# Partition sums issued four steps into a stage, squares added in two steps, each bank's residual ahead of the previous bank's low parts, and head squares taken a bank at a time

## The chip, the cores and the metric

The kernel runs on one core of a Trainium2 chip. The engines are named as in the profile: PE is TensorE (PEld its weight loads), DVE VectorE, ACT ScalarE, POOL GpSimd and SP SyncE, which issues most of the DMAs. The metric is the device time of one execution in microseconds (us). The median of the runs before is compared with that of the runs after.

## What is computed

The reference is a trunk of four layers on 256 positions of width 1024, in float32. Cut to what matters:

```python
for i in range(DEPTH):                       # 4 layers
    h = _rmsnorm(x, norm1[i])
    m = (retention, moba, diff)[i % 3](h)    # layers 0 and 3 are retention
    x = x + m
    x = x + _squared_relu_mlp(_rmsnorm(x, norm2[i]), w_up[i], w_down[i])

def _rmsnorm(x, w):
    return x * lax.rsqrt(jnp.mean(x * x, axis=-1, keepdims=True) + EPS) * w
```

The two attention mixers normalise queries and keys per head; the differential one (layer 2) also normalises each head's output of 128 columns. The retention mixer projects to queries, keys, values and a gate.

## The kernel before

The residual stream stays in the core's memory as `X`, with features on the 128 partitions: 8 chunks of 128 features by 256 positions. Every weight is streamed from HBM once, in raw tiles of 1 MB, each cut into two pieces. To keep float32 accuracy at the speed of the `fp32r` type, each operand is split in a high part (ACT copies it to `fp32r`: `whi`, `xhi`) and a low part (DVE subtracts the high part: `wlo`, `xlo`), and a product is three matmuls, high x high, high x low, low x high (`passes`, lines 333 to 335). A piece takes 12 matmuls of 512 columns (`mm_b`) or 24 of 256 columns (`mm_a`, `mm_o`).

`advance` splits pieces ahead of their use: when piece n is taken, the pieces up to n+4 have been put on ACT's and DVE's queues. Every engine works through its queue in program order, so where a step is issued decides what stands in front of it. Small steps are put off by hand: `later(n, f)` runs `f` at the n-th `tick` from now, and a tick comes once per piece, and once more inside the first piece of a stage.

There are eight norms, one ahead of each mixer (`norm1`) and one ahead of each MLP (`norm2`). A norm is spread over the border of two stages:

- `finish` ends a stage. PE completes the four PSUM banks `acc` one after the other; for each bank DVE adds it to `X` (behind an MLP it first scales it by `r2b` into `sc`), ACT writes `xhi` of its two chunks and DVE `xlo` (`norm_part`), and ACT squares the two chunks into a tile `sq` (`squares`). The new stage's matmuls work on `xhi` and `xlo` without the norm's factor, which is a number per position and is multiplied in later.
- `rms`, one tick into the next stage, adds the four `sq` tiles on DVE and then the two halves of the sum.
- `rms_sum`, one tick later, sums over the partitions by a matmul with ones into the PSUM tile `ms`. For an MLP DVE turns it into `r2b` (lines 316 and 317), which is used when that MLP finishes. For a mixer DVE makes `me` and its reciprocal `r2`, and POOL the inverse square root `r` in 13 small steps (`rsqrt`).

In the attention layers `qk_norm` needs `me` (through the POOL step `qem`). It makes sums of squares per head (DVE's `TENSOR_REDUCE`), POOL makes the factors `qf`, DVE scales the queries (`qn`), and PE transposes them (`qkT`) when the second group of four pieces is done. In layer 2 `av_diff` makes the outputs of four pairs of heads in two PSUM banks (`od`); ACT takes the squares and their sums over each 128 columns, eight instructions with an accumulator each, and POOL makes factors of them.

Of the kernel before, what the change touches and what calls it, by code (L numbers as in the profile page):

```python
# [9 lines left out]
F32 = mybir.dt.float32  # L10
F32R = mybir.dt.float32r
I32 = mybir.dt.int32
AF = mybir.ActivationFunctionType
OP = mybir.AluOpType
AX = mybir.AxisListType

P = 128
# [14 lines left out]
def trunk(ctx, tc, x_t, cols, rel_bias, w_up, w_down, ret_w_in, ret_w_out, moba_w_in, moba_w_out,  # L32
# [3 lines left out]
    PE, ACT, DVE, POOL = nc.tensor, nc.scalar, nc.vector, nc.gpsimd  # L36
# [7 lines left out]
    mp = ctx.enter_context(tc.tile_pool(name="mp", bufs=1))  # L44
# [21 lines left out]
    def later(n, fn, *a):  # L66
        clock[1] += 1
        pending.append((clock[0] + n, ORDER.get(fn.__name__, 3), clock[1], fn, a))

    def run_due():  # L70
        while True:
            due = [p for p in pending if p[0] <= clock[0]]
            if not due:
                return
            p = min(due, key=lambda p: p[:3])
            pending.remove(p)
            p[3](*p[4])

    def tick():
        clock[0] += 1  # L80
        run_due()
# [4 lines left out]
    def hi_lo(i, a, b, narrow):  # L86
        n = a * b
        hi = wp.tile([P, n], F32R, tag="hi", name="whi", bufs=NPC)
        odd = i % 2
        lo = wp.tile([P, n + (32 if odd else 96)], F32R, tag="lo%d" % (i % NPC), name="wlo", bufs=1)  # L90
        o = 0 if odd == narrow else (32 if odd else 96)
        return (t.rearrange("p (a b) -> p a b", a=a) for t in (hi, lo[:, o:o + n]))
# [35 lines left out]
    for l in range(DEPTH):  # L128
        j = l // 3
# [20 lines left out]
    def load_raw(part=0, of=1):  # L150
        i = nxt[0]
        if i >= len(specs):
            return
        src, a, b = specs[i]
        if part == 0:
            raws[i] = rp.tile([P, a, b], F32, tag="raw", name="raw", bufs=NRAW)
        hs = slice(part * (a // of), (part + 1) * (a // of))
        nc.sync.dma_start(raws[i][:, hs, :], src[:, hs, :])
        if part == of - 1:
            nxt[0] += 1  # L160
# [40 lines left out]
    def take():  # L201
        p = pieces.pop(nxt[2])
        nxt[2] += 1
        return p
# [13 lines left out]
    junk = const.tile([P, 512], mybir.dt.bfloat16, name="junk")  # L218
# [40 lines left out]
    def wn(l, which, k):  # L259
        c = 32 * which + l * KC + k  # L260
        return W[:, c:c + 1]
# [18 lines left out]
    st = {}  # L280
# [7 lines left out]
        st["hi"] = hi[:, oh:oh + n].rearrange("p (k s) -> p k s", k=KC)  # L288
        st["lo"] = lo[:, ol:ol + n].rearrange("p (k s) -> p k s", k=KC)

    def norm_part(l, which, q):

        for k in (2 * q, 2 * q + 1):
            ACT.activation(st["hi"][:, k, :], X[:, k, :], AF.Copy, scale=wn(l, which, k))
        for k in (2 * q, 2 * q + 1):
            DVE.scalar_tensor_tensor(st["lo"][:, k, :], X[:, k, :], wn(l, which, k),  # L296
                                     st["hi"][:, k, :].bitcast(F32), op0=OP.mult, op1=OP.subtract)

    def squares(q):
        sq = mp.tile([P, 512], F32, tag="pe", name="sq", bufs=9)  # L300
        ACT.activation(sq, X[:, 2 * q:2 * q + 2, :].rearrange("p k s -> p (k s)"), AF.Square)
        st["sq", q] = sq

    def rms(which):

        ss = st["sq", 0]
        for q in range(1, 4):
            DVE.tensor_tensor(ss, ss, st["sq", q], op=OP.add)
        DVE.tensor_tensor(ss[:, :S], ss[:, :S], ss[:, S:], op=OP.add)
        later(1, rms_sum, which, ss)  # L310

    def rms_sum(which, ss):
        ps = aux_bank("ms")
# [37 lines left out]
    def first_qk(ps):  # L351

        for i in range(2):
            pieces[i] = tuple(hi_lo(i, 4, S, True))

        def turn(pr):
            norm_part(0, 0, pr)
            hi, lo = pieces[pr // 2]
            kk = slice(pr % 2 * 2, pr % 2 * 2 + 2)
            raw = raws[0][:, 2 * pr:2 * pr + 2, :]  # L360
            ACT.activation(hi[:, kk], raw, AF.Copy)
            DVE.tensor_tensor(lo[:, kk], raw, hi[:, kk].bitcast(F32), op=OP.subtract)

        def meet(pr):

            ks = (2 * pr, 2 * pr + 1)
            hi, lo = pieces[pr // 2]
            for k in ks:
                for m in range(2):
                    mc = slice(m * P, (m + 1) * P)  # L370
                    pc = ps[:, m * S:(m + 1) * S]
                    PE.matmul(pc, lhsT=hi[:, k % 4, mc], rhs=st["hi"][:, k, :], start=k == 0 and m == 0, stop=False,
                              skip_group_check=True)
                    PE.matmul(pc, lhsT=hi[:, k % 4, mc], rhs=st["lo"][:, k, :], start=False, stop=False,
                              skip_group_check=True)
            for k in ks:
                for m in range(2):
                    mc = slice(m * P, (m + 1) * P)
                    PE.matmul(ps[:, m * S:(m + 1) * S], lhsT=lo[:, k % 4, mc], rhs=st["hi"][:, k, :], start=False,
                              stop=k == KC - 1 and m == 1, skip_group_check=True)  # L380

        turn(0)
        turn(1)
        for pr in range(4):
            meet(pr)
            if pr == 3:
                for q in range(4):
                    squares(q)
            if pr < 2:
                turn(pr + 2)  # L390
            if pr == 2:
                nxt[1] = nxt[2] = nxt[3] = 2
                load_raw()
                for _ in range(2):
                    split_piece()
                    split_lo()
            if pr:
                tick()
        for i in range(2):
            pieces.pop(i)  # L400
# [32 lines left out]
    def finish(srcs, mlp_out, nxt_norm):  # L433
        advance(4, 4)
        pcs = [take() for _ in srcs]
        if nxt_norm is not None:
            norm_new(nxt_norm[1] == 1)
        for q in range(4):
            for i, (pc, src) in enumerate(zip(pcs, srcs)):
                for c in (2 * q, 2 * q + 1):  # L440
                    mm_o(c, pc, src, False, i == len(srcs) - 1)
            xs = X[:, 2 * q:2 * q + 2, :]
            ps = st["acc"][q].rearrange("p (k s) -> p k s", k=2)
            if mlp_out:
                sc = mp.tile([P, 2, S], F32, tag="t2k", name="sc", bufs=4)
                DVE.tensor_tensor(sc, ps, r2b.unsqueeze(1).to_broadcast([P, 2, S]), op=OP.mult)
                DVE.tensor_tensor(xs, xs, sc, op=OP.add)
            else:
                DVE.tensor_tensor(xs, ps, xs, op=OP.add)
            if nxt_norm is None:  # L450
                nc.sync.dma_start(out.rearrange("(k p) s -> p k s", p=P)[:, 2 * q:2 * q + 2, :], xs)
            else:
                norm_part(nxt_norm[0], nxt_norm[1], q)
                squares(q)
            tick()
        if nxt_norm is not None:
            later(1, rms, nxt_norm[1])
# [194 lines left out]
    def attention(l):  # L652
# [139 lines left out]
        def av_diff(b):  # L792
            so = small("so", [P, 4, 2])
            sums = small("s1", [P, 4, 2])
            banks = []
            for i in range(4):
                p = b * 4 + i
                if i % 2 == 0:
                    banks.append(aux_bank("od").rearrange("p (i q v) -> p i q v", i=2, q=2))
                ps = banks[-1][:, i % 2]  # L800
                s = PT[p][0]
                vs = slice(p * P, (p + 1) * P)
                PE.matmul(ps[:, 0], lhsT=s[:, 0:P], rhs=V[0][:, vs], start=True, stop=True)
                PE.matmul(ps[:, 1], lhsT=s[:, P:S], rhs=V[0][:, vs], start=True, stop=False)
                PE.matmul(ps[:, 1], lhsT=s[:, S:GL], rhs=V[1][:, vs], start=False, stop=True)
                if i % 2 == 1:
                    for j in (i - 1, i):
                        for qt in range(2):
                            ACT.activation(junk[:, :P], banks[-1][:, j % 2, qt], AF.Square,
                                           accum_out=so[:, j, qt:qt + 1])  # L810
                POOL.tensor_copy(sums[:, i, :], SM[p][:, :, 0])
            m = small("om", [P, 4, 2])
            POOL.tensor_tensor(m, sums, sums, op=OP.mult)
            POOL.tensor_scalar(m, m, EPS, None, op0=OP.mult)
            POOL.tensor_scalar(so, so, 1.0 / P, None, op0=OP.mult)
            POOL.tensor_tensor(m, m, so, op=OP.add)
            f = small("of", [P, 4, 2])
            rsqrt(f, m, "of", POOL)
            later(2, od_scale, b, banks, f)
# [100 lines left out]
```

## Time and profile before

| | |
|---|---|
| median of 3 runs | 1374.78 us (1373.95 to 1375.21) |
| the profiled execution | 1373.68 us |
| its span, first to last instruction | 1371.9 us |
| PE busy | 1331.1 us, 97% of the span |
| DVE, ACT, POOL busy | 868.2, 684.9, 110.7 us |
| DMA traffic | 242.53 MB, mean 177 GB/s |

The profile shows one execution; its time lies 1.1 us under the median of the runs, and 1.8 us lie outside its span. Busy time counts a matmul from its start to its modelled end, and matmuls overlap, so that a busy PE may still be running slowly: the granted clock, in shares of full speed, says whether it does.

### The profile page before, as it was taken

To read this page: it belongs to the slowest core of one execution; us is meant where nothing else is said; L and a number is where in the kernel's file an instruction comes from. 1 tells how busy PE (TensorE), PEld (TensorE's weight loads), DVE (VectorE), ACT (ScalarE), POOL (GpSimd) and SP (SyncE) were. 2 spreads that over 40 slices of the span, in tenths; PEclk is the share of its full clock that TensorE was granted. 3 is DMA by queue.
4 is the path that set the end of the run, shared out by engine and by line. 5 is a ranking of instruction groups with operands and counts; after the bars stand their busy time and mean duration, and the time that the engine had idled before them with its cause. 6 is when DMAs were issued, how large, how long until landed. Compare 5 with 4: busy or idle time off the path is not lost.

```text
span 1371.9 us, 23860 instructions
## 1 busy us (share of the span) xinstructions
PE 1331.1 (97%) x10035; PEld 1249.1 (91%) x10035; DVE 868.2 (63%) x1237; ACT 684.9 (50%) x1002; POOL 110.7 (8%) x295
## 2 busy tenths in 40 slices
PE   8999999999989999999989999999899999999998
PEld 6888899999977789999967789999888889999998
DVE  7666647555577857555568676555666665665555
ACT  5454435444445754444456754544445444454442
POOL 1111100000041000000031100000030111000000
PEclk9999999999999999999999999999999999999999
DMA  8544554555554336555543337555555545365551
GB/s 299 166 167 162 186 185 167 203 204 195 185 197 141 123 128 215 185 192 203 190 144 133 123 126 243 184 185 186 176 167 171 184 157 195 115 236 203 202 184 63
DMA packets 141691, 242.53 MB, mean 177 GB/s; under 512 B 4160, under 2 KB 89824, under 8 KB 141584
## 3 DMA queue, kind: packets, MB, share of 16 engines
q1 hardware_dynamic: 139760, 237.78, 50.5%
q0 software_dynamic: 752, 2.33, 0.6%
q8 instruction: 78, 1.28, 0.4%
q10 hardware_dynamic: 1072, 0.90, 0.2%
q14 instruction: 29, 0.24, 0.1%
HBM read 239.92 MB, written 1.07 MB: 176 GB/s over the span
## 4 chain that ended last, share of the span: by engine, by line
PE 88%; DVE 6%; ACT 3%; DMA 1%; issue 1%; SPq 0%; DVEq 0%; ACTq 0%
PE acc L333 10%; PE acc L334 10%; PE acc L335 10%; PE up L335 8%; PE up L333 8%; PE up L334 8%; PE vg L333 4%; PE vg L335 4%; PE vg L334 4%; PE qkv L333 3%; PE qkv L334 3%; PE qkv L335 3%; PE qk L333 2%; PE qk L334 2%; PE qk L335 2%; DVE xlo L296 2%
## 5 line engine op out<-in xcount | busy, mean ns | idle before, releaser
L186 DVE TENSOR_TENSOR wlo<-raw,whi 128x1024 fp32r<-128x1024 f32 (+1 forms) x448 | 526.9, 1215 | 96.6 <-ACT whi L176 95.5
L176 ACT ACTIVATE whi<-raw 128x1024 fp32r<-128x1024 f32 (+1 forms) x448 | 451.9, 1052 | 94.1 <-PE acc L334 58.1
L335 PE MATMUL up<-xhi,wlo 128*128 128x256 f32 x1024 | 283.8, 277 | 1.2 <-DVE wlo L186 1.2
L333 PE MATMUL up<-xhi,whi 128*128 128x256 f32 x1024 | 284.3, 278 | 0.0
L334 PE MATMUL up<-xlo,whi 128*128 128x256 f32 x1024 | 283.4, 277 | 0.0
L334 PE MATMUL acc<-uu,whi 128*128 128x256 f32 x1024 | 282.7, 276 | 0.0
L333 PE MATMUL acc<-uu,whi 128*128 128x256 f32 x1024 | 282.6, 276 | 0.0
L335 PE MATMUL acc<-uu,wlo 128*128 128x256 f32 x1024 | 282.6, 276 | 0.0
L335 PEld LDWEIGHTS up<-xhi,wlo 128*128 128x128 f32 x1024 | 193.0, 188 | 1.8 <-DVE wlo L186 1.8
L334 PEld LDWEIGHTS up<-xlo,whi 128*128 128x128 f32 x1024 | 193.1, 189 | 0.1
L333 PEld LDWEIGHTS up<-xhi,whi 128*128 128x128 f32 x1024 | 193.0, 188 | 0.1
L333 PEld LDWEIGHTS acc<-uu,whi 128*128 128x128 f32 x1024 | 192.2, 188 | 0.0
L335 PEld LDWEIGHTS acc<-uu,wlo 128*128 128x128 f32 x1024 | 192.2, 188 | 0.0
L334 PEld LDWEIGHTS acc<-uu,whi 128*128 128x128 f32 x1024 | 192.2, 188 | 0.0
L466 DVE SCALAR_TENSOR_TENSOR u<-up,u 128x512 f32<-128x512 f32 x64 | 44.2, 690 | 207.4 <-ACT u L465 207.4
L465 ACT ACTIVATE u<-up 128x512 f32<-128x512 f32 x64 | 38.3, 599 | 255.7 <-PE up L335 255.7
L333 PE MATMUL acc<-oh,whi 128*128 128x256 f32 x384 | 106.9, 278 | 0.0
L334 PE MATMUL acc<-ol,whi 128*128 128x256 f32 x384 | 106.1, 276 | 0.0
L335 PE MATMUL acc<-oh,wlo 128*128 128x256 f32 x384 | 106.1, 276 | 0.0
L333 PE MATMUL vg<-whi,xhi 128*128 128x512 f32 x256 | 100.5, 393 | 0.0
L335 PE MATMUL vg<-whi,xlo 128*128 128x512 f32 x256 | 99.7, 390 | 0.0
L334 PE MATMUL vg<-wlo,xhi 128*128 128x512 f32 x256 | 99.7, 390 | 0.0
(220 smaller groups left out, 1931.3 us busy)
## 6 DMA issues: line engine op xcount, KB each, us to landing
raw<-in_w_up_dram SPq DMA_DIRECT2D x64, 1024.0 KB, 5.4
raw<-in_w_down_dram SPq DMA_DIRECT2D x64, 1024.0 KB, 5.7
raw<-in_ret_w_in_dram SPq DMA_DIRECT2D x45, 1024.0 KB, 5.2
raw<-in_ret_w_out_dram SPq DMA_DIRECT2D x16, 1024.0 KB, 4.8
raw<-in_moba_w_in_dram SPq DMA_DIRECT2D x12, 1024.0 KB, 5.2
raw<-in_diff_w_in_dram SPq DMA_DIRECT2D x12, 1024.0 KB, 5.2
raw<-in_moba_w_out_dram SPq DMA_DIRECT2D x4, 1024.0 KB, 4.9
raw<-in_diff_w_out_dram SPq DMA_DIRECT2D x4, 1024.0 KB, 4.9
```

Source lines behind the costliest of these rows:

```text
L176: ACT.activation(hi[:, part], half[:, part], AF.Copy)
L186: DVE.tensor_tensor(lo[:, part], half[:, part], hi[:, part].bitcast(F32), op=OP.subtract)
L296: DVE.scalar_tensor_tensor(st["lo"][:, k, :], X[:, k, :], wn(l, which, k), st["hi"][:, k, :].bitcast(F32), op0=OP.mult, op1=OP.subtract)
L333: PE.matmul(ps, lhsT=ah, rhs=bh, start=first, stop=False, skip_group_check=True)
L334: PE.matmul(ps, lhsT=ah, rhs=bl, start=False, stop=False, skip_group_check=True)
L335: PE.matmul(ps, lhsT=al, rhs=bh, start=False, stop=last, skip_group_check=True)
L465: ACT.activation(u, ps, AF.Relu)
L466: DVE.scalar_tensor_tensor(u, ps, 0.0, u, op0=OP.max, op1=OP.mult)
```

## The change

The change has four parts, in five places of the code. (1) `rms_sum` is issued two ticks later, at the fourth tick of a stage in place of the second. (2) `rms` adds three of the four tiles of squares; the last one and the two halves are added a tick later, by the new `rms_fold`. (3) `norm_part` is cut in `norm_hi` and `norm_lo`, and in `finish` the low parts of a bank are issued behind the residual of the next bank. (4) `av_diff` squares a whole bank on ACT with no accumulator, and DVE sums each 128 columns.

```diff
-    def norm_part(l, which, q):
+    def norm_hi(l, which, q):
 
         for k in (2 * q, 2 * q + 1):
             ACT.activation(st["hi"][:, k, :], X[:, k, :], AF.Copy, scale=wn(l, which, k))
+
+    def norm_lo(l, which, q):
         for k in (2 * q, 2 * q + 1):
             DVE.scalar_tensor_tensor(st["lo"][:, k, :], X[:, k, :], wn(l, which, k),
                                      st["hi"][:, k, :].bitcast(F32), op0=OP.mult, op1=OP.subtract)
@@
         ss = st["sq", 0]
-        for q in range(1, 4):
+        for q in (1, 2):
             DVE.tensor_tensor(ss, ss, st["sq", q], op=OP.add)
+        later(1, rms_fold, which, ss)
+
+    def rms_fold(which, ss):
+        DVE.tensor_tensor(ss, ss, st["sq", 3], op=OP.add)
         DVE.tensor_tensor(ss[:, :S], ss[:, :S], ss[:, S:], op=OP.add)
-        later(1, rms_sum, which, ss)
+        later(2, rms_sum, which, ss)
@@
             else:
-                norm_part(nxt_norm[0], nxt_norm[1], q)
+                norm_hi(*nxt_norm, q)
+                if q:
+                    norm_lo(*nxt_norm, q - 1)
                 squares(q)
+                if q == 3:
+                    norm_lo(*nxt_norm, q)
             tick()
@@
                 if i % 2 == 1:
-                    for j in (i - 1, i):
-                        for qt in range(2):
-                            ACT.activation(junk[:, :P], banks[-1][:, j % 2, qt], AF.Square,
-                                           accum_out=so[:, j, qt:qt + 1])
+                    sq = mp.tile([P, 512], F32, tag="t2k", name="sq", bufs=4)
+                    ACT.activation(sq, banks[-1].rearrange("p i q v -> p (i q v)"), AF.Square)
+                    DVE.tensor_reduce(so[:, i - 1:i + 1, :].rearrange("p i q -> p (i q)"),
+                                      sq.rearrange("p (h d) -> p h d", d=P), axis=AX.X, op=OP.add)
```

How the instructions move is shown at three places. First, PE's queue at the start of layer 1's attention. The number behind `whi` tells the piece: 3967 is the first of the stage, 3995 the second. Before:

```order
L333 MATMUL qkv_4139<-whi_3967,xhi_4002 128x512
L334 MATMUL qkv_4139<-wlo_3968,xhi_4002 128x512
L335 MATMUL qkv_4139<-whi_3967,xlo_4001 128x512
L320 MATMUL ms_4156<-ones_90,sq_4028 128x1 x2
L333 MATMUL qkv_4138<-whi_3995,xhi_4002 128x512
L334 MATMUL qkv_4138<-wlo_3996,xhi_4002 128x512
```

And of the change, where `whi_4156` is the third piece of the stage and `whi_4160` the fourth:

```order
L339 MATMUL qkv_4139<-whi_4156,xhi_4002 128x512
L340 MATMUL qkv_4139<-wlo_4157,xhi_4002 128x512
L341 MATMUL qkv_4139<-whi_4156,xlo_4001 128x512
L326 MATMUL ms_4204<-ones_90,sq_4026 128x1 x2
L339 MATMUL qkv_4138<-whi_4160,xhi_4002 128x512
L340 MATMUL qkv_4138<-wlo_4161,xhi_4002 128x512
```

The sum over the partitions stood behind 12 matmuls of the stage and stands behind 36. In the stages that begin with `mm_a` (the MLPs and layer 3) it stood behind 24 matmuls and stands behind 72; in layer 0's mixer it moves 36 matmuls back.

Second, DVE's queue from the last two banks of layer 0's MLP to the start of layer 1's attention. Before:

```order
L446 TENSOR_TENSOR sc<-acc,r2b 128x512
L447 TENSOR_TENSOR X<-X,sc 128x512
L296 SCALAR_TENSOR_TENSOR xlo<-X,W,xhi 128x256 x2
L446 TENSOR_TENSOR sc<-acc,r2b 128x512
L447 TENSOR_TENSOR X<-X,sc 128x512
L296 SCALAR_TENSOR_TENSOR xlo<-X,W,xhi 128x256 x2
L630 TENSOR_TENSOR gs<-gps,msk 16x384
L308 TENSOR_TENSOR sq<-sq 128x512 x3
L309 TENSOR_TENSOR sq<-sq 128x256
L323 TENSOR_SCALAR me<-ms 128x2
L326 RECIPROCAL r_4161<-me 128x2
L186 TENSOR_TENSOR wlo<-raw,whi 128x1024 x6
```

And of the change:

```order
L298 SCALAR_TENSOR_TENSOR xlo<-X,W,xhi 128x256 x2
L453 TENSOR_TENSOR sc<-acc,r2b 128x512
L454 TENSOR_TENSOR X<-X,sc 128x512
L298 SCALAR_TENSOR_TENSOR xlo<-X,W,xhi 128x256 x4
L641 TENSOR_TENSOR gs<-gps,msk 16x384
L310 TENSOR_TENSOR sq<-sq 128x512 x2
L314 TENSOR_TENSOR sq<-sq 128x512
L315 TENSOR_TENSOR sq<-sq 128x256
L186 TENSOR_TENSOR wlo<-raw,whi 128x1024 x5
L329 TENSOR_SCALAR me<-ms 128x2
L332 RECIPROCAL r_4209<-me 128x2
L186 TENSOR_TENSOR wlo<-raw,whi 128x1024
```

The four additions of squares still stand between the last low parts of `X` and the first low part of a weight piece; `me` has moved behind five weight pieces.

Third, DVE's queue at the start of layer 0's MLP. Before:

```order
L296 SCALAR_TENSOR_TENSOR xlo<-X,W,xhi 128x256 x2
L308 TENSOR_TENSOR sq<-sq 128x512 x3
L309 TENSOR_TENSOR sq<-sq 128x256
L316 TENSOR_SCALAR r2b<-ms 128x256
L317 RECIPROCAL r2b<-r2b 128x256
L186 TENSOR_TENSOR wlo<-raw,whi 128x1024 x4
L466 SCALAR_TENSOR_TENSOR u<-up,u 128x512
L471 TENSOR_TENSOR uu<-u,uu 128x512
L186 TENSOR_TENSOR wlo<-raw,whi 128x1024 x2
```

And of the change:

```order
L310 TENSOR_TENSOR sq<-sq 128x512 x2
L314 TENSOR_TENSOR sq<-sq 128x512
L315 TENSOR_TENSOR sq<-sq 128x256
L186 TENSOR_TENSOR wlo<-raw,whi 128x1024 x4
L477 SCALAR_TENSOR_TENSOR u<-up,u 128x512
L482 TENSOR_TENSOR uu<-u,uu 128x512
L186 TENSOR_TENSOR wlo<-raw,whi 128x1024
L322 TENSOR_SCALAR r2b<-ms 128x256
L323 RECIPROCAL r2b<-r2b 128x256
L186 TENSOR_TENSOR wlo<-raw,whi 128x1024
```

The two steps of `r2b` have moved behind five weight pieces and behind the activation of the MLP's first group of units, `u` and `uu`.

## Rows read from the trace of the kernel before

**Rows 1.** The page: busy time, share of the span and instructions of PE.

```profile
PE 1331.1 (97%) x10035; PEld 1249.1 (91%) x10035; DVE 868.2 (63%) x1237; ACT 684.9 (50%) x1002; POOL 110.7 (8%) x295
```

**Rows 2.** PE's waits over the span: us in total, times, longest.

```profile
PE ms L320 <- DVE sq L309: 20.1, 4, 6.5
PE ms L315 <- DVE sq L309: 8.9, 4, 2.3
...
PE up L335 <- DVE wlo L186: 1.2, 3, 0.4
PE oT L831 <- ACT pT L770: 1.0, 1, 1.0
```

**Rows 3.** The windows view, five slow stretches: their length, busy times, granted clock, DMA.

```profile
1193.94:1197.33 3.39, 3.39 (x18) 3.39 (x17) 3.35 (x4) 0.25 (x1) 0.00 (x0) 0.51 0.00 0
sum 17.10, PE 17.10 PEld 15.59 DVE 17.02 ACT 3.61 POOL 9.55; mean PE 3.42 PEld 3.12 DVE 3.40 ACT 0.72 POOL 1.91
```

**Rows 4.** The windows view of a stretch in layer 1's MLP.

```profile
513.52:516.50 2.98, 2.98 (x27) 2.83 (x25) 2.86 (x3) 0.59 (x2) 0.00 (x0) 1.00 0.02 5
```

**Rows 5.** PE's timeline where stages begin: start, us, instruction [idle before <- releaser].

```profile
19.18 0.61 PE L320 MATMUL ms<-ones,sq 128*128 128x1 f32 x4 [2.99 <-DVE sq L309]
...
384.80 0.50 PE L333 MATMUL qkv<-whi,xhi 128*128 128x512 f32 x1
...
414.96 0.39 PE L335 MATMUL qkv<-whi,xlo 128*128 128x512 f32 x1
415.19 1.03 PE L705 MATMUL qkT<-ident,qn 128*128 128x128 f32 x8
...
507.73 0.28 PE L333 MATMUL up<-xhi,whi 128*128 128x256 f32 x1
...
685.55 0.39 PE L333 MATMUL qkv<-whi,xhi 128*128 128x512 f32 x1
...
986.05 0.28 PE L333 MATMUL qk<-xhi,whi 128*128 128x256 f32 x1
```

**Rows 6.** DVE's timeline from the end of layer 0's MLP into layer 1.

```profile
378.54 0.68 DVE L446 TENSOR_TENSOR sc<-acc,r2b 128x512 f32<-128x512 f32 x1
...
380.53 0.89 DVE L296 SCALAR_TENSOR_TENSOR xlo<-X,W,xhi 128x256 fp32r<-128x256 f32 x2 [0.58 <-ACT xhi L294]
...
390.17 2.19 DVE L308 TENSOR_TENSOR sq<-sq 128x512 f32<-128x512 f32 x3
...
393.93 0.16 DVE L323 TENSOR_SCALAR me<-ms 128x2 f32<-128x2 f32 x1 [1.11 <-PE ms L320]
...
394.21 5.76 DVE L186 TENSOR_TENSOR wlo<-raw,whi 128x1024 fp32r<-128x1024 f32 x5
...
404.45 1.36 DVE L681 TENSOR_REDUCE qss<-sq 128x8 f32<-128x512 f32 x2 [3.06 <-ACT sq L680]
```

**Rows 7.** DVE's timeline in layer 0, layer 1's MLP, and layers 2 and 3.

```profile
21.03 3.49 DVE L186 TENSOR_TENSOR wlo<-raw,whi 128x1024 fp32r<-128x1024 f32 x3
...
510.08 2.21 DVE L308 TENSOR_TENSOR sq<-sq 128x512 f32<-128x512 f32 x3
...
692.33 2.13 DVE L308 TENSOR_TENSOR sq<-sq 128x512 f32<-128x512 f32 x3
...
770.68 1.23 DVE L186 TENSOR_TENSOR wlo<-raw,whi 128x1024 fp32r<-128x1024 f32 x1 [4.27 <-ACT whi L176]
...
991.79 2.21 DVE L308 TENSOR_TENSOR sq<-sq 128x512 f32<-128x512 f32 x3
```

**Rows 8.** POOL's timeline in layer 1: two steps of `r`, the last of `qf`.

```profile
396.71 1.05 POOL L271 TENSOR_TENSOR r_t<-r 128x2 f32<-128x2 f32 x1
...
402.10 0.20 POOL L278 TENSOR_TENSOR r<-r_t,r 128x2 f32<-128x2 f32 x1
...
411.46 0.22 POOL L278 TENSOR_TENSOR qf<-qf_t,qf 128x16 f32<-128x16 f32 x1
```

**Rows 9.** ACT's timeline in layer 2: the first of 16 head squares.

```profile
763.02 0.28 ACT L809 ACTIVATE junk<-od 128x128 bf16<-128x128 f32 x1 [1.25 <-PE od L805]
```

More of the change, by code (lines that the diff above doesn't have):

```diff
@@ L356, in turn @@
         def turn(pr):
-            norm_part(0, 0, pr)
+            norm_hi(0, 0, pr)
+            norm_lo(0, 0, pr)
             hi, lo = pieces[pr // 2]
```

## Prediction

> **What bounds the kernel now.** I read the page first, then PE's waits over the whole span, then the granted clock behind those waits, then the timelines of PE, DVE and POOL where a stage begins. PE is the bound: busy for 1331.1 us, 97% of the span [rows 1]. So only what PE loses counts, and it loses in two ways. It waits: 29.0 us in eight waits for the additions of the squares, four in front of a mixer (20.1) and four in front of an MLP (8.9), and little for anything else; three waits for a low weight part are 1.2 together, one for a bank in layer 2 is 1.0 [rows 2]. And it runs slowly afterwards. In five stretches the granted clock is about 0.5, the 1.2 GHz level, against 1.00, the 2.4 GHz level, inside an MLP [rows 3, 4]. All five begin right behind a wait on `ms`: the four in front of the mixers, which last 3.0 to 6.5 us, and one of the four of 2.2 to 2.3 us in front of an MLP; behind the other three PE stayed at full clock. The five stretches last 17.10 us, of which half, 8.55 us, is lost.
>
> A wait also costs a little more than its idle time. Inside a stage 27 matmuls start in 2.98 us, one each 0.11 us [rows 4], while one is listed with 0.28 us [rows 5]. The next could have started 0.17 us before the idle time is counted from. For the twelve waits above that is 2.0 us.
>
> **What the change removes.** If none of these waits were left, it would be 29.0 + 1.2 + 1.0 + 8.55 + 2.0 = 41.75 us. The `ms` matmuls themselves stay, only later.
>
> **What is late next.** The additions keep their place on DVE, in front of the first low weight part of the new stage. When a stage's second piece is taken, `advance` issues the low parts of the third to sixth; the first two are split already. So PE can now run through two pieces, and into the third up to its first matmul with a low weight: the second matmul of the piece in an attention layer, the third in an MLP. There it waits for the additions and one `wlo`. I work out both times for each stage.
>
> *Layer 1.* Behind an MLP DVE waited 0.58 us for `xhi` in each of the four banks [rows 6]. Now the next bank's scale and residual stand in that place, and behind the last residual the third bank's two low parts (0.89), so the additions start 4 x 0.58 = 2.3 us earlier: 390.17 - 2.3 = 387.9. They take 2.65, a `wlo` 5.76 / 5 = 1.15 [rows 6]: the low part is there at 391.7. PE starts the stage at 384.80, 512 columns take 0.23 (414.96 to 415.19), and 25 matmuls bring it to 390.55 [rows 5]. Wait: 1.15 us.
>
> *Layer 2.* In the same way 692.33 - 2.3 + 2.65 + 1.15 = 693.8 [rows 7], against 685.55 + 25 x 0.23 = 691.3 [rows 5]: 2.5 us.
>
> *Layer 3.* 991.79 - 2.3 + 2.65 + 1.15 = 993.3 [rows 7], against 986.05 + 50 x 0.113 = 991.7 [rows 5]: 1.6 us.
>
> *The four MLPs* (layer 1's stands for all). Behind a mixer the last residual waits for PE and not for DVE, and two more low parts now stand behind it; I put the additions 0.2 us later. 510.08 + 0.2 + 2.65 + 1.15 = 514.1 [rows 7], against 507.73 + 50 x 0.113 = 513.4 [rows 5]: 0.7 us each, 2.8 together.
>
> *Layer 0's mixer.* PE's idle time there began at 19.18 - 2.99 = 16.2 [rows 5]. PE now goes on with 24 matmuls of 256 columns to 18.9 and waits for a `wlo` that started at 21.03 [rows 7] and starts 1.1 us earlier, with one addition and the half-sum fewer in front of it (0.7 + 0.4): 19.9 + 1.15 = 21.1, a wait of 2.1. Here `ms` still waits as well, because the last addition stands behind three `wlo`: 19.9 + 3 x 1.15 + 1.1 = 24.5, against 21.1 + 11 x 0.23 = 23.6. Together 3.0 us.
>
> New waits: 1.15 + 2.5 + 1.6 + 2.8 + 3.0 = 11.05 us. These are differences of start times, so nothing is added for their ends.
>
> *The clock behind them.* Two of the new waits (2.1 and 2.5) are as long as the four old ones of 2.2, of which one was followed by a slow stretch of 3.39 us, worth 1.7 [rows 3]. The rest are shorter. The bounds are none and all five norms with over 1 us (8.5); I take one, 1.7 us.
>
> *Head squares.* ACT gives up sixteen squares with an accumulator, the first at 763.02 [rows 9], for four of a whole bank, so that the exponentials and copies queued behind them come about 1 us earlier; that is the 1.0 of the wait in layer 2, counted above (0 to 1.2). DVE gets four reductions of 0.68 (1.36 for two [rows 6]). They fall where DVE waited 4.27 us for ACT [rows 7], and I cost them at nothing; without that cover they cost up to 2.7. The Trainium skill (VectorE: DVE Perf Modes, Rules for kernel authors) speaks against this part: it calls `tensor_reduce` the slowest DVE operation and advises restructuring it where it is on the hot path. By that rule the sum would be 2.7 us smaller; by the row, which shows DVE waiting there, it is unchanged.
>
> *What else moves.* The low parts of a bank come one scale and one residual later, 1.4 us (378.54 to 380.53 less the 0.58 of idle [rows 6]): the first bank's are done at 382.2, and PE needs them at 384.80. `r2b` is wanted at the end of the MLP only. `me` comes later, at 391.7 + 4 x 1.15 = 396.3 instead of 393.93 [rows 6]; see the first rival. SP's DMAs wait for the `wlo` that empties a raw tile, and these now come earlier.
>
> **The sum.** 41.75 - 11.05 - 1.7 = 29.0 us. From the profiled execution's 1373.68 that gives 1344.7; the median of the runs lies 1.1 above it, so I predict 1345.8 us. Without a new slow stretch it is 1344.1.
>
> **Rivals.** *POOL takes over in layers 1 and 2.* `me` starts the chain `r` (13 steps), `qem`, `qf` (13 steps), `qn`, behind which PE transposes. PE reaches the transposes about 6.3 us earlier, at 408.9 instead of 415.19. In the old lengths the chain takes from 393.93 to 411.68 [rows 6, 8] and 0.7 for `qn`, 18.4 us, of which DVE spent 3.06 waiting for PE's squares [rows 6]. From 396.3 on, 15.4 us end at 411.7: a stall of 2.8 us, 5.6 in two layers, so 1351.4. Against it: a step of `r` took 1.05 us while five `wlo` ran on DVE and 0.20 afterwards [rows 6, 8], and now `me` stands behind those five, so that most steps should be short and the chain ready at about 408. The Trainium skill (GPSIMD Engine Reference, Specifications) says that GpSimd's memory interfaces are shared with VectorE and contended by instructions with two inputs in SBUF, as `wlo` is. By that rule too the steps behind the five `wlo` are short; the trace agrees, with 1.05 against 0.20 us.
>
> *The clock falls behind every new wait* of over 1 us: four more slow stretches of 1.7, so 1352.6. For it: one wait of 2.2 us was enough once. Against it: three of that length were not.
>
> *The wait moves on rather than going.* If DVE is later than I count, by another instruction or by ACT's high parts, PE waits twice as long at each new place: 11 us more, 1356.8. If all of it came back, the time would be the old one (no change); for that the first `wlo` would have to be 3 to 5 us later than worked out.
>
> *Slower than before.* The clock could stay down. A microsecond at 1.2 GHz costs half a microsecond, so if slow stretches lasted 58 us longer in all than I count, the gain would be gone, and from 64 us on the kernel would be slower by over 0.2%. The place would be behind the new waits in layers 0 and 2. Against it: the five slow stretches so far last 3.4 us on average (17.10 for five [rows 3]), and PE has more work and less idle time there than before.
>
> **How the numbers follow.** My forecast has 0.66 (1341 to 1349.5), POOL 0.10, the clock 0.10, the doubled waits 0.08, no change 0.03, slower 0.03. The range 1339 to 1354 takes in the first three cases and, at its lower end, new waits of half the length (1340.3) without a slow stretch (1338.6). Within 0.2%, about 2.7 us, is what a measurement of this kernel can't tell from no change. Faster by more: 0.94; within: 0.03; slower: 0.03.
>
> **What the new profile would show.** PE's waits: `ms` gone but for about 1 us in layer 0; in its place waits of PE for `wlo` on the eight stage starts, 0.7 to 2.5 us, about 10 in all. Fewer slow stretches, one or two in place of five. DVE without the 0.58 before `xlo`. In layers 1 and 2 no wait of PE at `qkT`; one there would mean the POOL rival. In layer 2 no wait at `oT`. The prediction is wrong if the waits for `wlo` come to over 20 us, or if PE starts to wait for `uu` or for a raw tile's DMA.

## The result, and the profile after

The change makes the kernel faster: 1341.12 us median (1340.11 to 1342.20), against 1374.76 us before on the same chip, a ratio of 0.9756 (95% interval 0.9739 to 0.9773). That is 33.6 us less, where 29.0 were forecast; 1345.8 was predicted with a range of 1339 to 1354. The profiled execution took 1341.73 us, with a span of 1339.9.

The page, busy time of PE, against [rows 1]:

```profile
PE 1321.6 (99%) x10035; PEld 1241.1 (93%) x10035; DVE 868.5 (65%) x1241; ACT 680.2 (51%) x974; POOL 102.0 (8%) x295
```

PE does the same 10035 matmuls and is busy 9.5 us less, since less of them runs at half clock; the rest of the 32.0 us by which the span is shorter is idle time that went. PE's waits, against [rows 2] (us in total, times, longest):

```profile
PE qkv L340 <- DVE wlo L186: 3.0, 2, 2.2
PE ms L326 <- DVE sq L315: 1.8, 1, 1.8
PE vg L340 <- DVE wlo L186: 1.8, 1, 1.8
PE up L341 <- DVE wlo L186: 1.7, 4, 0.4
PE hot L244 <- DVE warm L224: 1.3, 1, 1.3
PE qk L341 <- DVE wlo L186: 1.3, 2, 1.0
```

The sums over the partitions now wait once, in layer 0. In their place PE waits for a first low weight part `wlo` at each of the eight stages. Its timeline has them one by one (start, us, instruction, idle time before it and the releaser):

```profile
20.23 0.50 PE L340 MATMUL vg<-wlo,xhi 128*128 128x512 f32 x1 [1.76 <-DVE wlo L186]
24.80 0.61 PE L326 MATMUL ms<-ones,sq 128*128 128x1 f32 x4 [1.77 <-DVE sq L315]
212.58 0.39 PE L341 MATMUL up<-xhi,wlo 128*128 128x256 f32 x1 [0.42 <-DVE wlo L186]
389.23 0.50 PE L340 MATMUL qkv<-wlo,xhi 128*128 128x512 f32 x1 [0.78 <-DVE wlo L186]
681.87 0.50 PE L340 MATMUL qkv<-wlo,xhi 128*128 128x512 f32 x1 [2.24 <-DVE wlo L186]
757.78 0.48 PE L842 MATMUL oT<-ident,on 128*128 128x128 f32 x2 [0.26 <-ACT pT L781]
971.12 0.39 PE L341 MATMUL qk<-xhi,wlo 128*128 128x256 f32 x1 [1.03 <-DVE wlo L186]
```

Without the last wait but one, for `oT`, and with the other MLPs' 0.42 us, the idle time is 9.26 us (1.76 + 1.77 + 0.78 + 2.24 + 1.03 + 4 x 0.42). One stretch of PE is slow, behind the sum in layer 0, against five in [rows 3]. In the windows view of it the granted clock is the third number from the right:

```profile
26.37:29.36 2.99, 2.99 (x9) 2.32 (x7) 2.92 (x8) 0.00 (x0) 0.18 (x1) 0.50 0.75 241
```

DVE's timeline at layer 1's start answers to [rows 6]. The 0.58 us before `xlo` is gone, and the additions start 2.90 us after the stage (382.49) in place of 5.37:

```profile
383.34 1.67 DVE L298 SCALAR_TENSOR_TENSOR xlo<-X,W,xhi 128x256 fp32r<-128x256 f32 x4
384.93 0.54 DVE L641 TENSOR_TENSOR gs<-gps,msk 16x384 f32<-16x384 f32 x1
385.39 1.40 DVE L310 TENSOR_TENSOR sq<-sq 128x512 f32<-128x512 f32 x2
386.89 0.69 DVE L314 TENSOR_TENSOR sq<-sq 128x512 f32<-128x512 f32 x1
387.62 0.43 DVE L315 TENSOR_TENSOR sq<-sq 128x256 f32<-128x256 f32 x1
387.96 5.76 DVE L186 TENSOR_TENSOR wlo<-raw,whi 128x1024 fp32r<-128x1024 f32 x5
393.64 0.15 DVE L329 TENSOR_SCALAR me<-ms 128x2 f32<-128x2 f32 x1
```

The next table sets the stages of the two profiled executions side by side, each from its first matmul to that of the next stage. "Delay" is the idle time of the new waits with 0.17 us for each, the difference that the prediction counts between idle time and starts.

| stage | wait on the sum before | new delay, forecast | new delay, measured | stage shorter by |
|---|---|---|---|---|
| layer 0 mixer | 2.99 | 3.0 | 3.87 | -0.42 |
| layer 1 mixer | 5.05 | 1.15 | 0.95 | 6.91 |
| layer 2 mixer | 6.52 | 2.5 | 2.41 | 7.77 |
| layer 3 mixer | 5.55 | 1.6 | 1.20 | 6.60 |
| four MLPs | 8.9 | 2.8 | 2.4 | 2.42, 2.55, 2.53, 3.3 |
| sum | 29.0 | 11.05 | 10.8 | 31.7 |

(The slow stretches, the wait for `oT` and the waits that went with [rows 2]'s low parts are in the last column too.)

### The profile page after: what moved, and what is told of

Read it like the earlier page. It is cut to its first block, busy times and chain, and to the rows that moved or that the text cites. A ratio compares the mean times of both kernels' runs of the same rounds, so it can differ in the third digit from the quotient of the medians.

```text
span 1339.9 us, 23834 instructions
## 1 busy us (share of the span) xinstructions
PE 1321.6 (99%) x10035; PEld 1241.1 (93%) x10035; DVE 868.5 (65%) x1241; ACT 680.2 (51%) x974; POOL 102.0 (8%) x295
## 3 DMA queue, kind: packets, MB, share of 16 engines
HBM read 239.92 MB, written 1.07 MB: 180 GB/s over the span
## 4 chain that ended last, share of the span: by engine, by line
PE 93%; DVE 5%; DMA 1%; ACT 1%; issue 0%; SPq 0%; DVEq 0%; ACTq 0%
PE acc L339 12%; PE acc L341 12%; PE acc L340 12%; PE up L341 8%; PE up L339 8%; PE up L340 8%; PE vg L339 4%; PE vg L340 4%; PE vg L341 4%; PE qkv L339 3%; PE qkv L340 3%; PE qkv L341 3%; PE qk L341 2%; PE qk L339 2%; PE qk L340 2%; DVE xlo L298 1%
```

## The experiments

Theory A is the prediction's: each part is worth the time by which it moves DVE's additions or PE's need of them, and the new waits are nothing but the order of DVE's queue. The rivals say that a part is worth nothing alone, that the head squares cost what they save, that POOL's chain or the weight parts themselves are the next bound, or that a split step is what keeps layer 0 going.

### The parts alone

The first kernel is the one before with the new `av_diff` alone:

```diff
-                    for j in (i - 1, i):
...
+                    ACT.activation(sq, banks[-1].rearrange("p i q v -> p (i q v)"), AF.Square)
...
```

> Part 4 alone: the kernel before with the head squares taken a bank at a time. Theory A (the work that DVE takes over lies where it waited): the wait of 1.0 us for the transposes in layer 2 goes and perhaps 0.5 us at the second pair of heads; all else as before. 1.0 to 1.7 us faster, 1373.1 to 1373.8 us. Rival B (the four reductions are on DVE's path): up to 2.7 us slower, 1377.5 us, and new waits of PE in layer 2.

Measured: 1373.88 us against 1374.36, ratio 1.0001 (0.9992 to 1.0010). By time it can't be told from no change. By the trace theory A's mechanism is there. PE's wait for the transposes `oT` falls to 0.28 us, and no new wait of PE in layer 2 takes its place:

```profile
775.73 1.01 PE L831 MATMUL oT<-ident,on 128*128 128x128 f32 x4 [0.28 <-ACT pT L770]
```

Layer 2's mixer lasts 121.09 us in place of 122.70, 1.6 us less. Of this 0.77 is the wait and 0.45 the six transposes `pT` ahead of it, which start within 0.54 us in place of 0.99. The last 0.4 lies at the second four `oT`: the next matmul starts 0.36 us after the first of them, in place of 0.77. What this execution gained there it lost at the MLPs of layers 0 and 2, which were each 0.84 us longer, with a slow stretch behind their sums. Rival B's 2.7 us are not to be seen.

The second is the one before with the new order in `finish` alone:

```diff
-                norm_part(nxt_norm[0], nxt_norm[1], q)
+                norm_hi(*nxt_norm, q)
+                if q:
+                    norm_lo(*nxt_norm, q - 1)
                 squares(q)
+                if q == 3:
+                    norm_lo(*nxt_norm, q)
```

> Part 3 alone: the kernel before with the next bank's residual ahead of the low parts. Theory A (its worth is the time by which the additions start earlier): the additions in layers 1 to 3 start 2.5 us earlier after the stage's start, so PE's waits on the sums in front of these mixers fall from 5.05, 6.52 and 5.55 us to 2.5, 4.0 and 3.1 us; the waits in front of the MLPs and of layer 0 stay. 7.5 us faster, 1367.3 us, and up to 3 us more if a slow stretch goes with a wait. Rival C (the order of the low parts is worth something only beside the late sum): 1374 us, waits as before.

Measured: 1365.41 us, ratio 0.9938 (0.9925 to 0.9950), 9.0 us faster. PE's waits on the sums in front of the mixers of layers 1, 2 and 3 are 2.60, 4.06 and 3.09 us, each 2.45 us shorter than before, as theory A has it; the four in front of the MLPs stay (9.1 us in place of 8.9):

```profile
PE ms L322 <- DVE sq L311: 12.7, 4, 4.1
PE ms L317 <- DVE sq L311: 9.1, 4, 2.3
```

The profiled executions differ by 7.25 us, near the 7.5 expected; the median moved 1.5 us more. Rival C falls.

The third is the one before with the new `rms` and `rms_fold` alone:

```diff
-        for q in range(1, 4):
+        for q in (1, 2):
...
-        later(1, rms_sum, which, ss)
+        later(2, rms_sum, which, ss)
```

> Parts 1 and 2 alone: the sum over the partitions at the fourth step and the squares added in two steps, low parts in the old order, head squares as before. Theory A: the waits for the first low weight part in layers 1 to 3 are 2.5 us longer than in the changed kernel (3.2, 4.7 and 3.5 us in place of 0.8, 2.2 and 1.0), and the 1.2 us of the head squares are missing: 1349.8 us. If a wait of over 3 us brings the slow clock whatever it is for, three stretches worth 1.3 to 2.1 us each come on top: 1355 us. Rival C (low parts without worth): 1342.3 us.

Measured: 1353.04 us, ratio 0.9849 (0.9836 to 0.9862), between the two sizes of theory A, and 10.7 us from rival C's. In the profiled execution the granted clock was 0.50 behind two of the three waits for `wlo`, those in layers 1 and 2 (2.71 and 2.57 us), and 1.00 behind that in layer 3 (1.55 us). PE's waits:

```profile
PE qkv L338 <- DVE wlo L186: 5.3, 2, 2.7
PE qkv L337 <- ACT whi L176: 2.1, 2, 1.9
PE ms L324 <- DVE sq L313: 1.9, 1, 1.9
PE qk L339 <- DVE wlo L186: 1.8, 2, 1.5
```

In layers 1 to 3 the idle time is 2.97, 4.43 and 2.78 us (3.2, 4.7 and 3.5 expected). Part of it has a releaser that I had not named: in layer 2 1.86 us for the high part `whi`, and in layer 3 1.23 us for `xhi`. ACT's timeline shows why in layer 2:

```profile
680.78 0.91 ACT L294 ACTIVATE xhi<-X,W 128x256 fp32r<-128x256 f32 x2 [1.36 <-DVE X L451]
681.60 0.61 ACT L301 ACTIVATE sq<-X 128x512 f32<-128x512 f32 x1
682.65 0.20 ACT L649 ACTIVATE ld<-ld 128x2 f32<-128x2 f32 x1 [0.44 <-DVE junk L647]
682.76 3.89 ACT L176 ACTIVATE whi<-raw 128x1024 fp32r<-128x1024 f32 x4
```

With the low parts in the old order each residual on DVE comes late, ACT waits 1.36 us for every one, and its weight parts stand behind the last. So the new order of low parts brings DVE's additions and ACT's high parts forward together.

The three parts alone gain 0.5, 9.0 and 21.3 us, 30.8 in sum; the whole change gains 32 to 34. If one part needs or hinders another, that is within the 1 to 3 us by which these two differ, and such a sum can't show it.

### Part 2, the additions in one step

```diff
-        for q in (1, 2):
+        for q in (1, 2, 3):
             DVE.tensor_tensor(ss, ss, st["sq", q], op=OP.add)
-        later(1, rms_fold, which, ss)
-
-    def rms_fold(which, ss):
-        DVE.tensor_tensor(ss, ss, st["sq", 3], op=OP.add)
         DVE.tensor_tensor(ss[:, :S], ss[:, :S], ss[:, S:], op=OP.add)
-        later(2, rms_sum, which, ss)
+        later(3, rms_sum, which, ss)
```

> The changed kernel without part 2: all additions in one step, the sum still at the fourth step of the stage. Only layer 0 differs. Theory A: there the last addition no longer stands behind three low weight parts, so PE's wait of 1.8 us on the sum goes, and the first low weight part comes 1.1 us later (wait 2.9 us in place of 1.8): 0.7 us faster, 1340.4 us, and 1.9 us more where the slow stretch behind the sum goes with it. Rival D (the split is what keeps layer 0 going; without it DVE's rotary step and the weight parts behind it are late): 1 to 3 us slower, 1342 to 1344 us.

Measured: 1342.84 us, ratio 0.9774 (0.9761 to 0.9787), which overlaps the changed kernel's interval. The wait on the sum in layer 0 is gone, as theory A says, and that for `wlo` is 2.32 us (2.9 expected). Layer 0's mixer took 200.04 us; in seven executions with the changed kernel's layer 0 (the three of the changed kernel and four of kernels below) it took 198.98 to 201.17. So what the split is worth in layer 0 can't be told from how these differ. The 1.6 us that this execution lost lie elsewhere, in layer 2, where a wait of 2.26 us for `wlo` was followed by a slow stretch:

```profile
682.29:685.27 2.98, 2.98 (x8) 2.34 (x7) 2.98 (x4) 0.69 (x1) 0.00 (x0) 0.50 0.55 137
```

The wait is the same as the changed kernel's 2.24, behind which the clock stayed at 1.00. The time lies in rival D's range, but the loss is not in layer 0, where rival D looks for it. What part 2 alone is worth stays open.

### Taking the new waits away

The changed kernel was run again, with no edit, beside the next three.

> The changed kernel once more, beside the next three on one chip. Theory A: 1341.1 us, the waits within 0.1 us of those in its profile (0.78, 2.24, 1.03 and four of 0.42 us for a low weight part, 1.8 and 1.8 in layer 0). If the slow stretches fell by chance and not behind a given wait, their number or place differs while the waits stay: one to three of them, 1.0 to 2.1 us each.

Measured: 1341.31 us, ratio 0.9767 (0.9754 to 0.9780). All waits in layers 1 to 3 are within 0.02 us of the first profile, but in layer 0 the slow stretch stood behind the wait for `wlo` and not behind the sum, and the wait on the sum was 0.42 us in place of 1.77, since PE, running slowly, came to it later:

```profile
21.45:24.44 2.99, 2.99 (x9) 2.31 (x7) 1.62 (x3) 2.00 (x2) 0.00 (x0) 0.50 0.62 197
```

The second kernel issues the additions later:

```diff
-            later(1, rms, nxt_norm[1])
+            later(3, rms, nxt_norm[1])
...
-        later(1, rms_fold, which, ss)
+        if first:
+            later(1, rms_fold, which, ss)
+        else:
+            rms_fold(which, ss)
```

> The changed kernel with the additions of the squares behind the stage's first four low weight parts (two steps later, the sum at the fifth step); layer 0's mixer as it is. Theory A (the new waits are DVE's order and nothing else): the seven waits for a low weight part in layers 1 to 3 and the MLPs go, 5.7 us; the sum in layer 2 waits 0.6 us. PE then reaches the transposes of layers 1 and 2 earlier by 0.8 and 2.2 us, where they had a slack of 0.5 us behind POOL's factors, and waits there 0.3 to 1.2 and 1.7 us. Together 2.6 us faster than the changed kernel, 1338.5 us. Rival E (the weight parts themselves are late, by ACT's high parts or a raw tile's DMA): the waits stay at 0.4 us or more each with another releaser, 1341 us.

Measured: 1343.73 us, 2.4 us slower than the run above, where 2.6 faster was expected. The half that explains the waits holds: those for `wlo` are gone in layers 1 and 3 and the MLPs, and 0.43 us in layer 2, so rival E falls. But others came:

```profile
PE qkT L719 <- DVE qn L709: 2.3, 2, 1.3
PE ms L329 <- DVE sq L318: 1.9, 2, 1.4
PE vg L343 <- DVE wlo L186: 1.8, 1, 1.8
PE acc L343 <- DVE uu L485: 1.4, 4, 0.3
PE acc L342 <- ACT uu L484: 1.3, 4, 0.3
```

The wait at `qkT` was expected (1.01 and 1.31 us). The last two lines were not. In an MLP the late additions stand on DVE in front of the first activation, so PE waits for `uu`, twice 0.33 us, and each MLP is 0.5 us longer than with the 0.42 us wait that went. Another 1.0 us of the difference between the profiled executions lies in layer 0, where the code is the same and only the slow stretch stands elsewhere (behind the sum).

```diff
+        later(7 if st.get("att") else 0, rms_root, me)
+
+    def rms_root(me):
         r = small("r", [P, 2])
         rsqrt(r, me, "r", POOL)
         st["r"] = r
```

(`st["att"]` is set in `attention` and cleared in `mlp`.)

> The kernel above with POOL's inverse square root of the norm put off by seven steps in the attention layers, so that the factors of the queries are made first. Theory A (POOL's chain of 13 steps for the norm is what makes the transposes wait): no wait at the transposes, 2.0 to 2.9 us faster than the kernel above, 1336.1 us. Rival F (the factors are late because DVE's squares and sums are, not POOL): the waits at the transposes stay, 1338.5 us.

Measured: 1340.13 us, ratio 0.9756 (0.9743 to 0.9769), 3.6 us faster than the kernel above. No wait at `qkT` is left. The mixers of layers 1 and 2 are 1.4 and 1.7 us shorter than there, 3.1 together; layer 0's was shorter too in this execution, by 1.6, with the same code. So POOL's 13 steps for the norm were what held the transposes, and rival F falls.

```diff
-    later(3, rms, 0, True)
+    later(4, rms, 0)
...
-        later(2, rms_sum, which, ss)
+        later(2 if st.get("on") else 3, rms_sum, which, ss)
+        st["on"] = True
```

> The kernel above with layer 0's mixer changed in the same way: its additions in one step behind three low weight parts, its sum one step later. Theory A: the waits of 1.8 and 1.8 us there go but for some 0.4 us, 3.2 us faster than the kernel above, 1332.9 us, and 1.4 us more where a slow stretch goes too. Rival G (in layer 0 the DMA sets the time: its queues are full from 14 to 20 us): PE waits as long for a high part or a raw tile, 1336 us.

Measured: 1342.11 us, 2.0 us slower than the kernel above; both theories missed the time. The wait for `wlo` fell to 0.39 us, but PE's timeline has two others:

```profile
26.10 0.61 PE L327 MATMUL ms<-ones,sq 128*128 128x1 f32 x4 [1.66 <-DVE sq L315]
28.99 0.77 PE L543 MATMUL s<-qk 128*128 128x256 f32 x1 [2.28 <-DVE qk L534]
```

On DVE the additions stood behind a weight part that itself waited 2.29 us for ACT, and the rotary steps `qk` behind the additions. ACT in turn waited for a raw tile, so the DMA of rival G is there, one step further back (first ACT's line, then DVE's):

```profile
21.21 2.02 ACT L176 ACTIVATE whi<-raw 128x1024 fp32r<-128x1024 f32 x2 [2.63 <-DMA raw<-in_ret_w_in_dram]
...
22.31 1.23 DVE L186 TENSOR_TENSOR wlo<-raw,whi 128x1024 fp32r<-128x1024 f32 x1 [2.29 <-ACT whi L176]
23.45 1.41 DVE L310 TENSOR_TENSOR sq<-sq 128x512 f32<-128x512 f32 x2
24.90 0.69 DVE L314 TENSOR_TENSOR sq<-sq 128x512 f32<-128x512 f32 x1
...
28.76 0.42 DVE L535 TENSOR_TENSOR qk<-rb__330,ra 128x256 f32<-128x256 f32 x1
```

In layer 0 an addition done early fills time in which DVE would wait for ACT; done late, it makes the rotary step late. Layer 0's mixer is 3.8 us longer than in the kernel above. The waits named make 2.6 of it, and behind the last of them PE ran 5.96 us at a clock of 0.50, where the kernel above had 3.41 us at 0.50:

```profile
28.99:34.95 5.96, 5.96 (x16) 4.93 (x17) 4.73 (x9) 2.25 (x3) 2.67 (x9) 0.50 0.84 275
```

### The best placing of each, and the head squares once more

The changed kernel ran a third time, with no edit, as the measure of the next three.

> The changed kernel a third time, as the measure of the next three on one chip. Theory A: 1341.2 us, waits as in its profile; one slow stretch or two, whose place may be another one again.

Measured: 1341.93 us, ratio 0.9767 (0.9753 to 0.9780). Waits in layers 1 to 3 as before; one slow stretch in layer 0, of 6.7 us. It began behind the wait for `wlo` (1.78 us), and the granted clock stayed at 0.50 across the wait on the sum (0.33 us):

```profile
22.11:24.30 2.19, 2.19 (x6) 1.33 (x4) 1.83 (x3) 1.61 (x3) 0.00 (x0) 0.50 0.67 163
24.30:26.23 1.93, 1.60 (x7) 1.36 (x6) 1.93 (x3) 1.64 (x2) 0.00 (x0) 0.50 0.99 383
26.23:28.79 2.56, 2.56 (x8) 1.98 (x6) 2.53 (x5) 0.00 (x0) 0.00 (x0) 0.50 0.63 196
```

The next kernel has the new `av_diff` taken back:

```diff
-                    ACT.activation(sq, banks[-1].rearrange("p i q v -> p (i q v)"), AF.Square)
...
+                    for j in (i - 1, i):
...
```

> The changed kernel without part 4 (ACT squares and sums each 128 columns again). Theory A: the wait of about 1.0 us for the transposes in layer 2 comes back, 0.8 to 1.6 us slower than the changed kernel, 1342.0 to 1342.8 us. Rival B (the four reductions on DVE cost what ACT saves): no difference, 1341.2 us, with a wait taken away elsewhere in layer 2.

Measured: 1342.85 us, ratio 0.9781 (0.9765 to 0.9798), 0.9 us above the changed kernel beside it, which is within what these runs tell apart. The wait is back, and layer 2's mixer is 1.68 us longer:

```profile
757.40 0.30 PE L842 MATMUL oT<-ident,on 128*128 128x128 f32 x1 [1.05 <-ACT pT L781]
```

With the first kernel's 1.6 us this shows part 4's worth on PE twice, and rival B falls by the trace, though not by time. In this execution no stretch in layer 0 was slow, though the wait for `wlo` there was 1.76 us again:

```profile
21.09:24.59 3.50, 2.83 (x11) 1.99 (x11) 3.39 (x5) 2.57 (x3) 0.00 (x0) 1.00 0.66 195
```

```diff
-            later(1, rms, nxt_norm[1])
+            later(3 - 2 * nxt_norm[1], rms, nxt_norm[1])
...
-        later(1, rms_fold, which, ss)
+        if first or which == 1:
+            later(1, rms_fold, which, ss)
+        else:
+            rms_fold(which, ss)
```

(with `rms_root` as above, and `first` set in layer 0.)

> The changed kernel with late additions and the deferred root in front of the mixers of layers 1 to 3 alone; in front of the MLPs and in layer 0 as it is. Theory A (late additions save the wait for the first low weight part, and lose 0.5 us in each MLP because there the activation stands behind them): layers 1, 2 and 3 gain 1.1, 1.2 and 1.0 us over the changed kernel, the MLPs nothing: 3.3 us faster, 1337.9 us. Rival H (the gain of the mixers comes back later in them): 1340 us.

Measured: 1338.69 us, ratio 0.9745 (0.9731 to 0.9758), 3.2 us less than the changed kernel beside it (1341.93). The mixers of layers 1, 2 and 3 are 1.0, 1.2 and 1.0 us shorter, the MLPs the same, and rival H falls. This is the fastest version that ran.

```diff
-            lambda_full()
+            later(6, lambda_full)
...
-        later(2, rms_sum, which, ss)
+        later(2 if st.get("on") else 3, rms_sum, which, ss)
+        st["on"] = True
```

> The kernel above, with layer 2's four small DVE steps for lambda put off by six steps, and layer 0's sum one step later. Theory A: in layer 2 the remaining waits of 0.43 us for a low weight part and 0.41 us for the sum go; in layer 0 the wait of 1.8 us on the sum goes, since one piece of 2.7 us lies in front of it: up to 2.6 us faster than the kernel above, 1335.3 us. Rival G (layer 0 is set by the raw tiles that come from HBM, and the wait only moves to the next weight part or to the scores): 0.8 us, 1337.1 us.

Measured: 1343.28 us, 4.6 us slower than the kernel above; the expectation is wrong for layer 2, and open for layer 0. There the wait on the sum is gone, with a slow stretch behind the wait for `wlo`, and the mixer took 199.05 us. But the kernel with the deferred root, with its sum in the old place and its slow stretch in the same one, had no wait on the sum either and took 199.11, so that the later sum has no worth of its own that these runs show. In layer 2 the wait for `wlo` went, the one on the sum stayed (0.38 us), and PE waited 4.42 us at `qkT`, because DVE, which makes `qn`, waited for the load of lambda:

```profile
695.06 0.23 DVE L662 SCALAR_TENSOR_TENSOR junk<-lam 128x64 bf16<-128x64 f32 x1 [7.38 <-DMA lam<-in_diff_lambda_dram]
```

`lambda_full` also issues that load, on POOL's queue. Put off, it stood behind the 13 steps of `qf` and was issued at 691.63, while DVE's steps that need it kept their place in front of `qn`. Behind this wait PE ran 5.88 us at a clock of 0.50 (698.65 to 704.53), and layer 2's mixer is 6.6 us longer in all. The fastest version with layer 0's later sum alone was not tried.

## Why the prediction was right, and where its sizes were off

**The mechanism.** It held at each step: the sums' waits went; the additions became PE's next limit through the first `wlo`, at all eight places; POOL did not take over; the head squares were hidden; the clock fell behind one of the new waits. That it was one was luck: with the same layer 0 it fell behind none in one later execution and for about twice as long in another.

**The new waits.** 11.05 us forecast, 10.8 measured in the same count. That the sums agree so closely is in part luck, since two errors cancel. Layers 1 to 3 and the MLPs were 0.1 to 0.4 us shorter than forecast each, 1.1 together. Layer 0 was 0.9 longer, by its wait on the sum (1.77 and 0.17 in place of 0.9): the prediction let DVE make three weight parts without a break, and the third waited 1.14 us for ACT, with the last addition behind it.

**The slow clock before was under-counted.** The step "The five stretches last 17.10 us, of which half, 8.55 us, is lost" is 2.05 us too small. I read the stretches from the second matmul behind the sum on; the windows of the kernel before, from the sum's first matmul to that point, show the clock already at 0.50 in three of the five:

```profile
392.88:394.33 1.45, 1.45 (x6) 1.35 (x7) 0.37 (x3) 1.45 (x2) 1.45 (x2) 0.50 0.00 0
694.97:696.42 1.45, 1.45 (x6) 1.35 (x6) 0.36 (x3) 1.45 (x2) 0.14 (x1) 0.50 0.00 0
994.60:995.80 1.20, 1.20 (x5) 1.20 (x6) 0.16 (x1) 1.20 (x3) 0.00 (x0) 0.50 0.01 3
```

That is 4.10 us at half clock, by the same halving 2.05 lost, an estimate. In the changed kernel's layer 0 the instructions of the first of these windows took 0.78 us at full clock (24.80 to 25.58) where they take 1.45 here, which bears it out.

**The head squares.** I gave the wait in layer 2 1.0 us, with bounds of 0 and 1.2. It was worth 1.6 to 1.7, since PE's six transposes ahead of the wait and the second four `oT` had been held up as well. DVE's reductions fall where it waits for ACT, as forecast:

```profile
745.82 0.69 DVE L820 TENSOR_REDUCE so<-sq 128x4 f32<-128x512 f32 x1 [2.06 <-ACT sq L819]
747.16 0.69 DVE L820 TENSOR_REDUCE so<-sq 128x4 f32<-128x512 f32 x1 [0.65 <-ACT sq L819]
```

The Trainium skill (VectorE: DVE Perf Modes, Rules for kernel authors) advises against `tensor_reduce` on the hot path. The trace does not contradict it: at 0.69 us each these four were not on it.

**POOL.** The rival did not come true, by half a microsecond. In layer 1 `qn` started at 404.81 and its first half was done near 405.45, and PE reached the transposes at 405.98. The late additions, with which PE came there about 1 us earlier, showed both the wait (1.01 and 1.31 us, where the rival said 2.8) and its cause. In the changed kernel's layer 1 the norm's steps took 0.19 to 0.20 us each but for the first, as the prediction argued, and in the factors' chain the long ones (1.10 and 1.07 us, at 401.34 and 402.52) fell while DVE made low weight parts from 401.15 on. The Trainium skill (GPSIMD Engine Reference, Specifications) says that the two engines share their memory interfaces; the trace agrees.

**The sum, made again.** 41.75 + 2.05 + 0.6 (head squares) - 10.8 - 1.5 (one slow stretch of 2.99 us) = 32.1 us; the two profiled executions differ by 1373.68 - 1341.73 = 31.95. The medians differ by 33.6, since the profiled execution of before lay 1.1 us below its median and that of after 0.6 us above it. So 1.7 of the 4.7 us by which the forecast missed is the choice of the executions, and 2.7 are the two terms above; the terms that were mis-sized are the slow clock before and the head squares.

## What to carry to other kernels

When a wait goes, find what stands behind the same work in the queue of the engine that was late, and compare start times there: outside layer 0 each new wait came out within 0.4 us. A step that is put off takes its loads and everything queued behind it along; the same delay of the additions gained 1.0 to 1.2 us in the mixers of layers 1 to 3 (with POOL's root put off as well) and lost 0.5 us in each MLP, so it must be priced stage by stage. And read a slow stretch from the first instruction behind the wait, small ones too.

## What was not expected of the hardware

The slow clock behind a wait is not fixed by the wait. In layer 0, with the same code, the granted clock was 0.50 for 2.99 us behind the sum in one execution, for 2.99 us behind the weight part in a second, from behind the weight part until 2.56 us of matmuls past the sum in a third, and at 1.00 throughout in a fourth. In layer 2 a wait of 2.24 to 2.26 us was followed by full clock in the changed kernel's three executions and by 2.98 us at 0.50 in the kernel with the additions in one step. The Trainium skill (TensorE: Matmul & The Clock Gate, Part 1) says that the point at which the clock first rises, at a kernel's start, varies between runs of one kernel; the traces show such a variation for its later falls, and what decides them here stays open.

What such a stretch costs depends on where it lies. Seven executions have the changed kernel's layer 0. From its sum's first matmul on, the mixer took 181.5 us in the three with the stretch behind the sum, 181.9 in the one with it on both sides, and 179.9 to 180.0 in the two with it in front of the sum and in the one without any. In front of the sum it filled time in which PE would have waited for DVE's additions, which were done 19.0 to 19.7 us into the stage in all seven. So behind the sum it cost 1.6 us, and in front nothing that shows. The runs of the changed kernel spread over 3.1 us (1340.11 to 1343.16).
